# High-half products first in each weight unit, and a sparser accumulating DMA, in a two-layer decoder step

## The chip, the cores and the metric

One core of a Trainium2 chip runs the whole program. The metric is the device time of one execution in microseconds; the kernel before took 1725.13 us as the median of 3 runs (1719.79 to 1726.79). The engines named below are TensorE (PE, its weight loads as PEld), VectorE (DVE), ScalarE (ACT), GpSimd (POOL) and SyncE (SP, which here only issues DMAs).

## The reference, cut to what matters

A step of a decoder with two layers and shared weights runs on 256 prompt tokens and 64 sample tokens, all float32, model width 1024, FFN width 2816:

```
for each layer:
    x = x + 0.5 * swiglu(rmsnorm(x), ffn1_w_gu, ffn1_w_down)
    h = rmsnorm(x)
    u, v, q, gates = split(h @ w_in)
    A = pooling mixer on u              # windows 2, 4, 8, 16, then a 256x256 map per group
    B = conv module on v                # GLU, depthwise conv of width 31, LayerNorm, swish, w_pw
    C = cross-attention of q            # keys and values: rmsnorm(mem) @ w_mem_kv, or a cache
    x = x + (sig(gA)*A + sig(gB)*B + sig(gC)*C) @ w_out
    x = x + 0.5 * swiglu(rmsnorm(x), ffn2_w_gu, ffn2_w_down)
y = rmsnorm(x)
```

Outputs are y for both groups, the new pooling and convolution states, and the memory keys and values of the prompt group.

## The kernel before, in words

**Layout.** Activations lie transposed: features on the 128 partitions, in 8 blocks, and the 256 + 64 = 320 tokens along the free dimension. A weight matrix is cut into blocks of 128 x 128, and the host has put all blocks of both layers into one array in the order of use, so that the kernel reads its weights as a stream. A piece of 16 blocks (1 MB) is one DMA of SP into a tile `raw`, of which there are four (`NRAW`). A piece is two units of 8 blocks, half 0 and half 1.

**Two halves of a number.** PE multiplies in fp32r, which keeps fewer bits than float32. So each float32 operand is cut into a high half, its fp32r rounding, and a low half, the rest, and a product is made of three: weight high by activation high, weight high by activation low, weight low by activation high. The activations' halves are `hhi` and `hlo` (after a norm), `hidh` and `hidl` (FFN hidden), `memh` and `meml` (memory tokens), `mgh` and `mgl` (merged branches) and `chi` and `clo` (convolution); the weights' halves are `whi` and `wlo`.

**Cutting the weights.** `Stream.split` (L211) makes both halves of a unit. The ordinary way (L224): ACT copies `raw` to `whi` with a cast, and DVE writes `wlo` as `raw - whi`; on the profile DVE's instructions carry the line of a helper, L116. The other way (L217 to L219): ACT copies, ACT writes `-raw` cast into `wlo`, and POOL issues a DMA that reads the same weights from HBM once more and adds them into `wlo`. This accumulating DMA is used while `share` is on, for half 1 of each piece: from the start of a layer's mixer to the end of its convolution, 37 of 73 units a layer, 74 of the program's 444 units. When half 1 is cut, the raw tile is given back, and SP may load into it.

**Look-ahead.** `Stream.unit` (L230) is called when PE's program reaches a unit u. It runs deferred work, cuts units up to u + 3 (`LA`), and advances side tasks (`pump`, L268). `whi` and `wlo` have four buffers each (`NW`), so the cut of a unit waits until PE has read the unit four before.

**Chains.** `chain` (L291) makes one output block of 128 features by 320 tokens in a PSUM bank: for each of its 8 blocks (22 in the down projection of the FFN) three matmuls, L294 (`whi` by high), L295 (`whi` by low), L296 (`wlo` by high). A unit of 8 blocks is 24 matmuls. `kv_values` (L456) makes the memory values with weights as the moving operand; there a unit is 12 matmuls of 512 columns at L469 to L471. PSUM has three banks `mm` for chains, two `cv` (shared with the convolution), two `st` and one `sa`; a chain waits until its bank has been read by DVE or ACT.

**Stages of a layer.** `ffn` (22 pairs of gate and up chains, then 8 down chains of 22 blocks); then `mixer`: the GLU projection (16 chains, whose results `za` and `sgv` DVE evicts), the memory keys (8 chains of 256 tokens, evicted by DVE into `kt`), the memory values, the queries, four groups of pooling projection, pool map, pooling gates and attention scores, then attention gates with attention values, convolution gates; then `w_pw` and `w_out`, and the second `ffn`. The last down chain of a stage gives the last of the 8 blocks of x, whose halves the next stage's first chain needs: DVE adds, ACT writes `hhi`, DVE writes `hlo`.

**Side tasks.** The depthwise convolution of the prompt tokens is 240 multiply-adds a layer on DVE (`cv`, two lanes), issued in slices of 2.5 steps a unit from the GLU projection on; for the sample tokens POOL does it. It must be done before `w_pw`. Softmax, pooling and the norms of the mixer are issued in such slices too.

**Order.** Each engine runs its queue in order. The tile framework fixes that order when the program is built: it takes instructions in program order as its own timing model finds them ready, so that a later instruction may be put before an earlier one that the model thinks would wait.

Of the kernel before, what the change touches and what calls it, by code (L numbers as in the profile page):

```python
# [11 lines left out]
ALU = mybir.AluOpType  # L12
# [3 lines left out]
P = 128  # L16
KB = 8
# [58 lines left out]
def trunk_kernel(  # L76
# [16 lines left out]
    nc = tc.nc  # L93
# [9 lines left out]
    clk = {"pe": 0.0, "dve": 0.0, "pool": 0.0}  # L103
# [19 lines left out]
    def nm(s):  # L123
        uid[0] += 1
        return f"{s}_{uid[0]}"
# [4 lines left out]
    def t320(s):  # L130
        return tp.tile([P, T], F32, name=nm(s), tag="t320", bufs=7)
# [4 lines left out]
    def pmm():  # L136
        return psum("mm", 3)
# [7 lines left out]
    def pst():  # L145
        return psum("st", 2)
# [18 lines left out]
    class Stream:  # L165
# [45 lines left out]
        def split(self, u):  # L211
            c, half = divmod(u, 2)
            raw = self.piece("w", c)[:, half * 1024:half * 1024 + 1024]
            hi = wp.tile([P, 1024], F32R, name=nm("whi"), tag="whi")
            lo = wp.tile([P, 1024], F32R, name=nm("wlo"), tag="wlo")
            if self.share and half == 1:
                nc.scalar.copy(hi[:, :], raw)  # L217
                nc.scalar.mul(lo[:, :], raw, -1.0)  # L218
                nc.gpsimd.dma_start(lo[:, :], w_in[c][:, 1024:2048], accum_op=ALU.add)  # L219
            else:  # L220
                n = 512 if u == 0 else 1024
                for e in range(0, 1024, n):
                    h, r = hi[:, e:e + n], raw[:, e:e + n]
                    nc.scalar.copy(h, r)  # L224
                    dve.tensor_tensor(out=lo[:, e:e + n], in0=r, in1=h.bitcast(F32), op=ALU.subtract)
            self.units[u] = (hi, lo)
            if half == 1:
                self.done("w", c)
# [60 lines left out]
    ws = Stream()  # L289

    def chain(out, xs, n):  # L291
        for i, (xh, xl) in enumerate(xs):
            hi, lo = ws.block()
            nc.tensor.matmul(out, hi, xh, start=(i == 0), stop=False)  # L294
            nc.tensor.matmul(out, hi, xl, start=False, stop=False)  # L295
            nc.tensor.matmul(out, lo, xh, start=False, stop=(i == len(xs) - 1))  # L296
            clk["pe"] += 3 * (3 + n / 2.4) * 1e-3


    def rsqrt_ops(ms, n, out, work=None):  # L300
# [60 lines left out]
    def ffn(h, mean, on_block):  # L361
# [12 lines left out]
        for j in range(NJ):  # L374
            pg = pwide()
            chain(pg[:, :T], xs, T)
            sg = t320("sg")

            def ev_gate(pg=pg, sg=sg):
                dve.tensor_tensor(out=sg[:, :], in0=pg[:, :T], in1=rstd[:, :], op=ALU.mult)  # L380
                nc.scalar.activation(sg[:, :], sg[:, :], AF.Silu)

            pu = pwide()
            if j == 0:
                chain(pu[:, :T], xs, T)
                ev_gate()
            else:
                ev_gate()
                chain(pu[:, :T], xs, T)
            up = t320("up")  # L390
            dve.tensor_tensor(out=up[:, :], in0=pu[:, :T], in1=rstd[:, :], op=ALU.mult)
            dve.tensor_tensor(out=up[:, :], in0=up[:, :], in1=sg[:, :], op=ALU.mult)

            def fin(j=j, up=up):
                split_plain(up[:, :], *ref(j))

            defer(fin)
# [58 lines left out]
    def kv_values(l, mh, vt):  # L456
        for half in range(2):
            pv = [pmm(), pmm()]
            for kp in range(4):
                assert ws.blk % 8 == 0  # L460
                hi, lo = ws.unit(ws.blk // 8)
                ws.blk += 8
                for kk in range(2):
                    k = 2 * kp + kk
                    wh, wl = hi[:, kk * 512:kk * 512 + 512], lo[:, kk * 512:kk * 512 + 512]
                    for mb in range(2):
                        sh = mh[0][:, k, mb * P:mb * P + P]
                        sl = mh[1][:, k, mb * P:mb * P + P]
                        nc.tensor.matmul(pv[mb][:, :], sh, wh, start=(k == 0), stop=False)  # L469
                        nc.tensor.matmul(pv[mb][:, :], sl, wh, start=False, stop=False)  # L470
                        nc.tensor.matmul(pv[mb][:, :], sh, wl, start=False, stop=(k == KB - 1))  # L471
                        clk["pe"] += 0.65
            for mb in range(2):
                nc.scalar.mul(vt[:, mb, half * 512:half * 512 + 512], pv[mb][:, :], rmcol[:, mb:mb + 1])
        nc.gpsimd.dma_start(mv_out[l], vt[:, :, :])
# [187 lines left out]
    def mixer(l, h, acc, on_block):  # L663
# [55 lines left out]
        start("norm", norm_gen(), 2)  # L719
        kv_keys(l, mh)  # L720
        kv_values(l, mh, vt)
        drain("norm")
        xs = hx(box[0])
# [168 lines left out]
    for l in range(L):  # L892
# [30 lines left out]
        else:  # L923
            fst = Stat()
            last = t320("sq")
# [9 lines left out]
    m = pst()  # L935
# [114 lines left out]
```

## Time and profile before

| | |
|---|---|
| median of 3 runs | 1725.13 us |
| profiled execution, whole / span | 1725.18 / 1723.4 us |
| PE busy | 1654.5 us (96%) |
| DVE busy | 1119.0 us (65%) |
| ACT busy | 840.7 us (49%) |
| POOL busy | 319.8 us (19%) |
| HBM read, written | 311.91 MB, 8.82 MB |

The span goes from the first to the last instruction; the profiled execution's own time is 1.8 us longer. Times in the views are microseconds from the span's start. In a row, `wlo<-raw,whi` says that an instruction writes `wlo` and reads `raw` and `whi`; `<-` in a list of waits stands between who waited and what ended the wait. Layer 0's mixer lies from about 253 to 580, layer 1's from about 1099 to 1430; the rest is FFN and projections.

### The profile page before, as it was taken

The page shows a single profiled execution, that of the slowest core. Times are in us where ns is not written, and L with a number is a line of the kernel's source. Part 1 is how long each engine was busy: PE and PEld are TensorE (multiplying, and loading weights), DVE is VectorE, ACT ScalarE, POOL GpSimd, SP SyncE. Part 2 cuts the span into 40 slices and gives each one's busy share as a digit, 9 for nine tenths or more (in the row PEclk, how much of TensorE's full clock was granted, in tenths as well). Part 3 has the DMA queues.
Part 4 walks back from the last instruction along what each step waited for, and adds up shares of the span by engine and source line. Part 5 has one row for each costly group of instructions (what it writes and reads, how often), then busy time and mean ns, then how long its engine had stood idle before and what let it go on. Part 6 is the DMA issues. An engine that isn't in the chain of part 4 may idle for free.

```text
span 1723.4 us, 27500 instructions
## 1 busy us (share of the span) xinstructions
PE 1654.5 (96%) x11194; PEld 1597.1 (93%) x11194; DVE 1119.0 (65%) x1822; ACT 840.7 (49%) x1267; POOL 319.8 (19%) x356
## 2 busy tenths in 40 slices
PE   8999998889999999999999999998899999999996
PEld 8999998879788999999999999997888899999996
DVE  7655449999754576564465555689995636755544
ACT  5444346656657354443344433555666664444432
POOL 2000005777410000000000000367762100000000
PEclk9999999999999999999999999999999999999999
DMA  7444457899899544444444444688888974444430
GB/s 266 147 147 152 152 185 214 219 256 253 251 293 273 176 151 155 147 147 148 147 147 150 153 155 154 180 230 230 227 266 269 311 208 161 147 150 154 155 129 31
DMA packets 51935, 322.52 MB, mean 187 GB/s; under 512 B 6240, under 2 KB 6304, under 8 KB 18656
## 3 DMA queue, kind: packets, MB, share of 16 engines
q1 hardware_dynamic: 38160, 270.75, 45.1%
q0 software_dynamic: 13360, 49.68, 13.5%
q8 instruction: 88, 1.44, 0.3%
q10 hardware_dynamic: 288, 0.33, 0.1%
q14 instruction: 39, 0.32, 0.1%
HBM read 311.91 MB, written 8.82 MB: 186 GB/s over the span
## 4 chain that ended last, share of the span: by engine, by line
PE 76%; DMA 9%; DVE 8%; issue 3%; POOL 2%; ACT 2%; DVEq 0%; SPq 0%; POOLq 0%; ACTq 0%
PE mm L296 17%; PE mm L294 17%; PE mm L295 17%; DMA wlo<-in_w 9%; PE cv L294 7%; PE cv L296 7%; PE cv L295 7%; DVE cv L116 3%; POOL pr L116 2%; DVE wlo L116 1%; PE sa L645 1%; DVE us L116 1%; PE st L825 1%; ACT wlo L218 1%; DVE hlo L116 0%
## 5 line engine op out<-in xcount | busy, mean ns | idle before, releaser
L224 ACT CAST whi<-raw 128x1024 fp32r<-128x1024 f32 (+1 forms) x371 | 388.3, 1047 | 601.5 <-PE mm L295 345.2
L116 DVE TENSOR_TENSOR wlo<-raw,whi 128x1024 fp32r<-128x1024 f32 (+1 forms) x371 | 465.3, 1254 | 242.5 <-ACT whi L224 241.6
L294 PE MATMUL mm<-hhi,whi 128*128 128x320 f32 x1736 | 547.0, 315 | 16.1 <-DVE sgv L116 9.6
L296 PE MATMUL mm<-hhi,wlo 128*128 128x320 f32 x1736 | 541.3, 313 | 16.4 <-DMA wlo<-in_w 16.3
L295 PE MATMUL mm<-hlo,whi 128*128 128x320 f32 x1736 | 542.0, 312 | 0.0
L294 PEld LDWEIGHTS mm<-hhi,whi 128*128 128x128 f32 x1736 | 329.3, 190 | 28.2 <-issue 15.5
L296 PEld LDWEIGHTS mm<-hhi,wlo 128*128 128x128 f32 x1736 | 328.9, 190 | 22.0 <-DMA wlo<-in_w 19.9
L295 PEld LDWEIGHTS mm<-hlo,whi 128*128 128x128 f32 x1736 | 329.4, 190 | 1.8 <-issue 0.4
L116 DVE SCALAR_TENSOR_TENSOR cv<-z,cst,cv 128x256 f32<-128x256 f32 x480 | 205.4, 478 | 3.4 <-ACT cv L484 1.4
L294 PE MATMUL cv<-hhi,whi 128*128 128x320 f32 x568 | 175.5, 309 | 0.0
L295 PE MATMUL cv<-hlo,whi 128*128 128x320 f32 x568 | 175.5, 309 | 0.0
L296 PE MATMUL cv<-hhi,wlo 128*128 128x320 f32 x568 | 175.5, 309 | 0.0
L116 POOL MEMSET z<- 128x120 f32 x4 | 0.8, 212 | 742.2 <-PE mm L295 742.2
L217 ACT CAST whi<-raw 128x1024 fp32r<-128x1024 f32 x74 | 77.5, 1048 | 120.3 <-PE mm L295 110.3
L294 PE MATMUL mm<-hidh,whi 128*128 128x320 f32 x418 | 129.2, 309 | 0.0
L295 PE MATMUL mm<-hidl,whi 128*128 128x320 f32 x418 | 129.2, 309 | 0.0
L296 PE MATMUL mm<-hidh,wlo 128*128 128x320 f32 x418 | 129.2, 309 | 0.0
L116 POOL TENSOR_TENSOR pr<-pr 128x512 f32<-128x512 f32 (+3 forms) x128 | 116.6, 911 | 6.6
L219 POOL DMA_DIRECT2D wlo<-in_w x74 | 64.6, 873 | 257.8 <-ACT wlo L218 188.5
L296 PEld LDWEIGHTS cv<-hhi,wlo 128*128 128x128 f32 x568 | 106.6, 188 | 0.0
L295 PEld LDWEIGHTS cv<-hlo,whi 128*128 128x128 f32 x568 | 106.6, 188 | 0.0
L294 PEld LDWEIGHTS cv<-hhi,whi 128*128 128x128 f32 x568 | 106.6, 188 | 0.0
(191 smaller groups left out, 2632.0 us busy)
## 6 DMA issues: line engine op xcount, KB each, us to landing
raw<-in_w SPq DMA_DIRECT2D x221, 1024.0 KB, 4.8
wlo<-in_w POOLq DMA_DIRECT2D x74, 512.0 KB, 8.9
raw<-in_kc SPq DMA_DIRECT2D x16, 1024.0 KB, 9.3
raw<-in_vc SPq DMA_DIRECT2D x16, 1024.0 KB, 8.7
out_co<-z POOLq DMA_DIRECT2D x16, 135.0 KB, 6.0
raw<-in_mem SPq DMA_DIRECT2D x2, 1024.0 KB, 4.8
out_mk<-kt POOLq DMA_DIRECT2D x2, 1024.0 KB, 9.4
out_mv<-va POOLq DMA_DIRECT2D x2, 1024.0 KB, 8.3
```

The costliest lines, as they stand in the source:

```text
L116: return op(*args, **kw)
L217: nc.scalar.copy(hi[:, :], raw)
L218: nc.scalar.mul(lo[:, :], raw, -1.0)
L219: nc.gpsimd.dma_start(lo[:, :], w_in[c][:, 1024:2048], accum_op=ALU.add)
L224: nc.scalar.copy(h, r)
L294: nc.tensor.matmul(out, hi, xh, start=(i == 0), stop=False)
L295: nc.tensor.matmul(out, hi, xl, start=False, stop=False)
L296: nc.tensor.matmul(out, lo, xh, start=False, stop=(i == len(xs) - 1))
L645: nc.tensor.matmul(po[32 * h:32 * h + 32, :256], pp[:, at:at + 32], raw[:, mb * 1024 + h * 256:mb * 1024 + h * 256 + 256], start=(bb == 0 ...
L825: nc.tensor.matmul(pv[:, :TP], vt[:, mb, o * P:o * P + P], kt[:, 2 * hd + mb, :], start=(mb == 0), stop=(mb == 1))
```

## The change

It has two parts. In `chain`, the blocks of one unit (or as many of them as belong to the chain) are taken together: first L294 and L295 for all of them, then L296 for all of them; `kv_values` does the same with its units. In `Stream.split`, the accumulating DMA is used, while `share` is on, for every unit whose number leaves 2 when divided by 3, whichever half it is, and no longer for each half 1.

```diff
--- before.py
+++ after.py
@@ -213,10 +213,10 @@
             raw = self.piece("w", c)[:, half * 1024:half * 1024 + 1024]
             hi = wp.tile([P, 1024], F32R, name=nm("whi"), tag="whi")
             lo = wp.tile([P, 1024], F32R, name=nm("wlo"), tag="wlo")
-            if self.share and half == 1:
+            if self.share and u % 3 == 2:
                 nc.scalar.copy(hi[:, :], raw)
                 nc.scalar.mul(lo[:, :], raw, -1.0)
-                nc.gpsimd.dma_start(lo[:, :], w_in[c][:, 1024:2048], accum_op=ALU.add)
+                nc.gpsimd.dma_start(lo[:, :], w_in[c][:, half * 1024:half * 1024 + 1024], accum_op=ALU.add)
             else:
                 n = 512 if u == 0 else 1024
                 for e in range(0, 1024, n):
@@ -289,12 +289,18 @@
     ws = Stream()
 
     def chain(out, xs, n):
-        for i, (xh, xl) in enumerate(xs):
-            hi, lo = ws.block()
-            nc.tensor.matmul(out, hi, xh, start=(i == 0), stop=False)
-            nc.tensor.matmul(out, hi, xl, start=False, stop=False)
-            nc.tensor.matmul(out, lo, xh, start=False, stop=(i == len(xs) - 1))
-            clk["pe"] += 3 * (3 + n / 2.4) * 1e-3
+
+        i, last = 0, len(xs) - 1
+        while i <= last:
+            m = min(8 - ws.blk % 8, last + 1 - i)
+            blocks = [(xs[i + e], ws.block()) for e in range(m)]
+            for e, ((xh, xl), (hi, lo)) in enumerate(blocks):
+                nc.tensor.matmul(out, hi, xh, start=(i + e == 0), stop=False)
+                nc.tensor.matmul(out, hi, xl, start=False, stop=False)
+            for e, ((xh, xl), (hi, lo)) in enumerate(blocks):
+                nc.tensor.matmul(out, lo, xh, start=False, stop=(i + e == last))
+            clk["pe"] += 3 * m * (3 + n / 2.4) * 1e-3
+            i += m
 
 
     def rsqrt_ops(ms, n, out, work=None):
@@ -460,16 +466,15 @@
                 assert ws.blk % 8 == 0
                 hi, lo = ws.unit(ws.blk // 8)
                 ws.blk += 8
-                for kk in range(2):
-                    k = 2 * kp + kk
-                    wh, wl = hi[:, kk * 512:kk * 512 + 512], lo[:, kk * 512:kk * 512 + 512]
-                    for mb in range(2):
-                        sh = mh[0][:, k, mb * P:mb * P + P]
-                        sl = mh[1][:, k, mb * P:mb * P + P]
-                        nc.tensor.matmul(pv[mb][:, :], sh, wh, start=(k == 0), stop=False)
-                        nc.tensor.matmul(pv[mb][:, :], sl, wh, start=False, stop=False)
-                        nc.tensor.matmul(pv[mb][:, :], sh, wl, start=False, stop=(k == KB - 1))
-                        clk["pe"] += 0.65
+                w4 = [(kk, mb) for kk in range(2) for mb in range(2)]
+                for kk, mb in w4:
+                    k, wh = 2 * kp + kk, hi[:, kk * 512:kk * 512 + 512]
+                    nc.tensor.matmul(pv[mb][:, :], mh[0][:, k, mb * P:mb * P + P], wh, start=(k == 0), stop=False)
+                    nc.tensor.matmul(pv[mb][:, :], mh[1][:, k, mb * P:mb * P + P], wh, start=False, stop=False)
+                for kk, mb in w4:
+                    k, wl = 2 * kp + kk, lo[:, kk * 512:kk * 512 + 512]
+                    nc.tensor.matmul(pv[mb][:, :], mh[0][:, k, mb * P:mb * P + P], wl, start=False, stop=(k == KB - 1))
+                    clk["pe"] += 0.65
             for mb in range(2):
                 nc.scalar.mul(vt[:, mb, half * 512:half * 512 + 512], pv[mb][:, :], rmcol[:, mb:mb + 1])
         nc.gpsimd.dma_start(mv_out[l], vt[:, :, :])
```

## Rows read from the trace of the kernel before

**Rows 1.** Windows by stage: busy us (instructions) per engine, clock, DMA share, GB/s.
```profile
253.00:372.00 119.00, 103.64 (x638) 96.79 (x637) 110.83 (x211) 70.57 (x110) 76.99 (x81) 0.94 0.81 219
372.00:580.00 208.00, 199.79 (x1422) 179.42 (x1421) 142.32 (x276) 132.05 (x233) 73.50 (x85) 1.00 0.89 263
580.00:1099.00 519.00, 519.00 (x3536) 518.52 (x3535) 302.58 (x428) 215.78 (x291) 2.83 (x5) 1.00 0.43 152
1099.00:1218.00 119.00, 101.58 (x631) 95.55 (x630) 109.51 (x202) 67.35 (x100) 79.39 (x85) 0.94 0.82 221
1218.00:1430.00 212.00, 202.87 (x1426) 182.77 (x1425) 139.78 (x267) 131.96 (x233) 71.45 (x76) 0.98 0.86 255
```

**Rows 2.** PE's waits from 253 to 372: total us, times, longest us.
```profile
PE mm L294 <- DVE sgv L116: 5.5, 2, 3.8
PE mm L296 <- DMA wlo<-in_w: 5.3, 4, 2.7
PE mm L471 <- DMA wlo<-in_w: 3.2, 1, 3.2
PE mm L294 <- DVE kt L116: 1.3, 1, 1.3
```

**Rows 3.** PE's waits from 372 to 580.
```profile
PE mm L296 <- DMA wlo<-in_w: 5.7, 5, 2.2
```

**Rows 4.** PE's waits from 1099 to 1218.
```profile
PE mm L296 <- DMA wlo<-in_w: 4.7, 2, 2.6
PE mm L294 <- DVE sgv L116: 4.0, 2, 3.8
PE mm L471 <- DMA wlo<-in_w: 3.3, 2, 2.2
PE mm L296 <- DVE wlo L116: 2.9, 1, 2.9
PE mm L294 <- DVE kt L116: 2.2, 1, 2.2
```

**Rows 5.** PE's waits from 1218 to 1430.
```profile
PE mm L296 <- DMA wlo<-in_w: 7.7, 6, 2.6
```

**Rows 6.** Windows on five stretches of lower granted clock.
```profile
326.10:329.50 3.40, 3.40 (x18) 3.40 (x17) 3.40 (x9) 1.65 (x3) 1.94 (x3) 0.50 1.02 222
356.80:363.60 6.80, 5.59 (x13) 4.38 (x14) 6.76 (x14) 3.83 (x7) 4.97 (x3) 0.50 0.66 183
...
1141.90:1145.20 3.30, 3.30 (x14) 3.30 (x13) 0.00 (x0) 0.00 (x0) 2.50 (x3) 0.50 0.94 228
1179.50:1186.20 6.70, 3.98 (x18) 3.98 (x19) 6.70 (x10) 0.00 (x0) 1.58 (x1) 0.50 0.74 214
1397.90:1404.70 6.80, 6.18 (x23) 6.18 (x24) 0.47 (x1) 0.18 (x1) 0.00 (x0) 0.50 0.82 212
```

**Rows 7.** Timeline of one accumulating unit: start us, us, engine, line, operation.
```profile
1388.16 0.85 POOL L219 DMA_DIRECT2D wlo<-in_w  x1 [13.49 <-ACT exo L653]
...
1398.52 0.63 PE L296 MATMUL mm<-hhi,wlo 128*128 128x320 f32 x1 [2.58 <-DMA wlo<-in_w]
```

**Rows 8.** Part 6 of the page, DMA issues: KB each, median us to landing.
```profile
wlo<-in_w POOLq DMA_DIRECT2D x74, 512.0 KB, 8.9
```

**Rows 9.** DVE groups, 253 to 372: count, busy us, mean ns, idle.
```profile
L116 DVE SCALAR_TENSOR_TENSOR cv<-z,cst,cv 128x256 f32<-128x256 f32 x126 | 54.4, 477 | 1.2 <-ACT cv L484 0.7
L116 DVE TENSOR_TENSOR wlo<-raw,whi 128x1024 fp32r<-128x1024 f32 x16 | 24.2, 1513 | 3.7 <-ACT whi L224 3.5
```

**Rows 10.** Groups of DVE from 20 to 250, the first FFN.
```profile
L116 DVE TENSOR_TENSOR wlo<-raw,whi 128x1024 fp32r<-128x1024 f32 x65 | 79.5, 1223 | 39.8 <-ACT whi L224 39.7
```

**Rows 11.** Groups of DVE from 1099 to 1218.
```profile
L116 DVE SCALAR_TENSOR_TENSOR cv<-z,cst,cv 128x256 f32<-128x256 f32 x134 | 57.1, 478 | 1.2 <-ACT cv L484 0.7
```

**Rows 12.** Timeline where the second FFN of layer 0 begins.
```profile
625.99 0.31 PE L294 MATMUL cv<-hhi,whi 128*128 128x320 f32 x1
...
628.33 0.55 DVE L116 SCALAR_TENSOR_TENSOR hlo<-x,cst,hhi 128x320 fp32r<-128x320 f32 x1
```


## The prediction

> **What bounds the kernel now.** I read the busy time by stage first, then who TensorE (PE) waited for in each stage, then the clock in the stretches after the long waits, then VectorE's (DVE's) costliest groups. By stage [rows 1] there are two kinds of time. In the FFN, and in the pointwise and output projections, PE is busy all of the time: 519.00 of 519.00 us, 3536 matmuls, 0.147 us from start to start. There nothing but PE's own work counts, and that work is the same after the change: same matmuls, same weight loads, other order. In the two mixers PE leaves holes. I cut each mixer in an early part (GLU projection, memory keys, memory values; 119 us each) and a late part (queries to the branch gates; 208 and 212 us). In the early parts DVE is the fullest engine beside PE, 110.83 and 109.51 of 119; in the late ones it has room, 142.32 of 208 and 139.78 of 212.
>
> The holes, by cause: the low half of a weight unit (wlo) that had not landed from its accumulating DMA cost 5.3 + 3.2 us in the first early part [rows 2], 5.7 in the first late part [rows 3], 4.7 + 3.3 in the second early part, where DVE's own wlo was 2.9 late as well [rows 4], and 7.7 in the second late part [rows 5]. That is 8.5, 5.7, 10.9 and 7.7: 32.8 us of waiting for a low half. The rest are evictions (sgv 5.5 and 4.0, kt 1.3 and 2.2), which the change does not touch directly.
>
> Such holes are paid twice. After several of them the granted clock is 0.50, which is 1.2 of 2.4 GHz [rows 6]: in the stretch at 1397.90, which follows the longest late wait, 23 matmuls took 6.18 busy us, 0.269 each against 0.147. So of 6.8 us at the low level about 45% is lost, 3.0 us.
>
> **The change part by part.**
>
> *Order inside a unit.* A unit of 8 blocks is now 16 products with the high half, then 8 with the low. Before, the first low product was third; now it is seventeenth: the low half may come 14 starts, 14 x 0.147 = 2.1 us, later. The last reader of the high half was the 23rd product, now it is the 16th: ScalarE's copy of the unit four ahead, which waits for that buffer, may start 7 starts, 1.0 us, earlier; its negated copy into wlo still waits for the low buffer, whose release does not move, but comes at once then. Together up to 3.1 us of slack for an accumulating unit. In one such unit [rows 7] POOL's issue took 0.85 us from 1388.16 and the low product came 10.4 us after it, 2.6 of them waited; the median from issue to landing is 8.9 us [rows 8]. For the key units (256 columns) I scale the cadence: 0.147 x 256/320 = 0.117, an estimate, so 1.6 + 0.8 = 2.4 us; for the value units (512 columns, 12 matmuls, low product from 3rd to 9th, high half free 3 starts earlier) 0.235, so 1.4 + 0.7 = 2.1 us. Against the longest waits, 2.7, 3.2 and 2.2 [rows 2, 4], about 1.5 us stays; the late ones, 2.6 at most [rows 5], are covered whole.
>
> *Every third unit.* From 37 accumulating units in a mixer to 24: 13 fewer each, 26 in all, so 13.3 MB less on the DMA queues (512 KB each [rows 8]), which are 0.81 to 0.89 busy there [rows 1], and 26 fewer POOL issues of 0.85 and as many ScalarE passes, both off the path. Instead DVE makes 26 more subtractions. The early part has 15 accumulating units of 32 before and 10 after: 5 more subtractions in each, at 1.51 us [rows 9], 7.5 us of DVE. The late part gets 8 more, about 10 us, into 66 or 72 us of DVE idle: nothing. Half-1 units that DVE now makes give their raw tile back after the subtraction rather than after ScalarE's pass, which moves SP's next load by a microsecond or two; the load has four raw tiles, seven units or some 24 us, and costs nothing.
>
> The early subtractions are dear: 1513 ns there [rows 9], 1223 in the FFN [rows 10], while POOL is busy 77 to 79 of 119 us there and nearly idle in the FFN [rows 1]. The Trainium skill (SBUF — State Buffer, Who interferes with whom) says that a DVE instruction with two SBUF inputs contends with a GpSimd instruction that reads SBUF, and both inputs of this subtraction are in SBUF; the trace agrees, and without that rule 5 of them would be 6.1 us and not 7.5.
>
> *Late parts.* All low waits go, 5.7 + 7.7 = 13.4 us, and the slow stretch at 1397.90 with them, 3.0: **16.4 us gained**. Bounds: half of it, 8 us, if waits for raw tiles or ScalarE come up behind; 16.4.
>
> *Early parts.* Low waits 8.5 + 10.9 less the 1.5 that stays are 17.9; the slow stretches after waits that contain a low half (3.40, 6.80, 3.30 and 6.70 us in [rows 6]) at 45% are 9.1. So PE alone would gain 27. But DVE sets the floor: 110.8 + 7.5 = 118.3 of today's 119 in the first, 109.5 + 7.5 = 117.0 in the second, before any idle. The convolution, which fills DVE's gaps, can be left for the late part as far as the low half's slack allows; the second mixer is a little ahead with it (134 steps against 126 at the end of the early part [rows 9, 11], 8 x 0.43 = 3.4 us). I take no gain in the first, 4 us in the second, **4 us**. Bounds: all 27, if DVE puts off its convolution; 15 lost, if both times 7.5 lands on the path.
>
> *Chains that begin a stage.* The last x block of a new stage is now wanted as products 15 and 16 of its first chain, not 22 and 23. In one such boundary [rows 12] the chain begins at 625.99, and the last hlo is ready at 628.33 + 0.55 = 628.88; PE would now ask for it at 625.99 + 15 x 0.147 = 628.19, 0.7 us early, where before it asked at 629.22. There are seven such boundaries and the program's start. PE may slip products of the next chain into that hole: between 0 and 8 x 0.7 = 5.6 us; I take **2 us lost**.
>
> *Sum.* 1725.2 (the profiled run, 1.8 us of it around its span of 1723.4) - 16.4 - 4 + 2 = 1706.8. The median of the runs is 1725.1, so no correction: **1707 us**, 1.1% faster. Its own range is 1697 to 1717.
>
> **The rivals.**
>
> *DVE becomes the bound of the early parts (slower).* Each high copy gets its subtraction late, keys wait for their PSUM bank longer than the 1.3 and 2.2 us of today [rows 2, 4]. For it: DVE at 93% there, and one DVE wlo already 2.9 late. Against: 9 us of its idle in each, and the convolution can wait. It decides when DVE's backlog passes what three PSUM banks bear, two key chains or 2 x 24 x 0.117 = 5.6 us; 7.5 us are added. Price: 15 us on the path, four more slow stretches of 6.8 us at 3.0 = 12, boundaries 5.6, against 16.4 in the late parts: 1725.2 + 15 + 12 + 5.6 - 16.4 = 1741.
>
> *Something else is late next (no change).* The low half waits no more, but raw tiles, ScalarE's copies and POOL's queue come out just behind it. For it: DMA 0.89 and 0.86 busy in the late parts [rows 1]. Against: 13 MB less traffic. Half of the late gain, nothing early: 1725.2 - 8 + 2 = 1719.
>
> *DVE has room (faster still).* The convolution drifts into the late parts and PE gets all: 1725.2 - 16.4 - 27 + 2 = 1684. For it: 66 and 72 us of DVE idle late. Against: DVE works in order, and the convolution's steps stand in its queue ahead of later subtractions.
>
> **How the numbers follow.** Forecast 0.46, no change 0.21, faster still 0.20, slower rival 0.13. About 0.5%, 8.6 us, is what a measurement here can tell from none. Faster by that (below 1716.5): nine tenths of the forecast, all of the faster rival, a fifth of the second: 0.66. Slower (above 1733.7): most of the slower rival, 0.12. Within: 0.22. The range leaves out a part of the rivals at either end: 1685 to 1730.
>
> **What would show it.** Right: waits of PE for DMA wlo under 5 us in all, no granted clock of 0.50 near the end of the second mixer, late parts of about 202 us each, DVE busier than 117 us in early parts that are no shorter than 115, FFN stages unchanged to 1 us. Wrong: late parts as long as before with another wait in place (then the second rival), early parts longer with waits for kt, sgv or DVE's wlo (the first), early parts near 105 us (the third), or holes of over 1 us where a stage begins.

## The result and the profile after

The kernel after took 1701.78 us (median of 4 runs, 1697.46 to 1705.72) against 1725.96 (4 runs): a ratio of 0.986 [0.983, 0.990]. The profiled execution took 1699.24 us, 25.9 less than that of before. The forecast of 1707 us was 5 us above the measured median. How the gain is made up is not what the prediction said, so that nearness is in good part luck.

The accumulating DMA in part 6 of the page after (KB each, median us to landing, as [rows 8]); 26 fewer, as reckoned, and sooner there (7.7 in a second profile of the same program, e7 below):

```profile
wlo<-in_w POOLq DMA_DIRECT2D x48, 512.0 KB, 7.0
```

For the stages I divided both traces where PE ends one and begins the next: GLU projection, keys with values, late part, then all between the mixers, and the first three again for the second mixer. The columns are those of [rows 1]. First after, then before, divided in the same way:

```profile
245.40:311.10 65.70, 59.55 (x391) 58.64 (x390) 59.41 (x108) 37.46 (x62) 29.22 (x33) 0.97 0.67 197
311.10:366.60 55.50, 50.16 (x292) 44.69 (x291) 51.64 (x93) 30.23 (x46) 35.63 (x37) 0.91 0.77 229
366.60:563.40 196.80, 189.03 (x1358) 171.82 (x1357) 157.15 (x293) 124.40 (x224) 80.07 (x84) 0.98 0.78 246
563.40:1085.40 522.00, 522.00 (x3558) 521.68 (x3557) 303.14 (x434) 216.18 (x293) 1.91 (x4) 1.00 0.43 151
1085.40:1148.80 63.40, 59.04 (x389) 58.27 (x388) 56.77 (x102) 34.55 (x54) 34.89 (x39) 0.97 0.69 204
1148.80:1200.70 51.90, 47.82 (x289) 41.99 (x288) 50.80 (x91) 30.87 (x47) 38.54 (x38) 0.97 0.82 245
1200.70:1393.90 193.20, 188.52 (x1357) 170.24 (x1356) 153.44 (x285) 123.81 (x221) 70.79 (x74) 0.99 0.79 250
```

```profile
245.60:312.60 67.00, 60.04 (x393) 58.84 (x392) 57.51 (x112) 39.62 (x65) 34.68 (x40) 0.97 0.79 216
312.60:376.00 63.40, 54.36 (x314) 47.87 (x312) 58.78 (x114) 37.20 (x53) 46.91 (x47) 0.92 0.84 227
376.00:569.10 193.10, 185.84 (x1333) 166.41 (x1334) 131.37 (x256) 125.06 (x224) 69.81 (x81) 1.00 0.89 263
569.10:1091.70 522.60, 522.29 (x3558) 521.70 (x3557) 308.12 (x435) 216.62 (x292) 1.92 (x4) 1.00 0.43 153
1091.70:1159.40 67.70, 60.96 (x389) 59.80 (x388) 55.13 (x109) 36.87 (x55) 39.55 (x45) 0.95 0.78 209
1159.40:1221.00 61.60, 50.91 (x308) 45.59 (x308) 58.78 (x104) 34.45 (x50) 40.75 (x41) 0.94 0.86 236
1221.00:1418.70 197.70, 189.28 (x1338) 169.74 (x1338) 129.82 (x251) 127.14 (x227) 71.45 (x76) 0.98 0.86 256
```

One trap lies in this division, and the matmul counts show it: the late parts have 1333 and 1338 matmuls before and 1358 and 1357 after. In the kernel before, a query chain's 24 and some 19 matmuls ran already among the values, at 0.147 us worth 3.5 and 2.8 us. At equal work the early parts (GLU to values) went from 130.4 - 3.5 = 126.9 to 121.2 and from 129.3 - 2.8 = 126.5 to 115.3: 5.7 and 11.2 us gained. The late parts went from 196.6 to 196.8 and from 200.5 to 193.2: 0.2 lost and 7.3 gained. The rest of the program is 1.9 shorter. Together 16.9 + 7.1 + 1.9 = 25.9.

These gains hold for this pair of executions. A second profile of the kernel after (e7) has early parts of 126.4 and 113.6 us and late parts of 197.2 and 193.7: 0.5 and 12.9 us gained early, 0.6 lost and 6.8 gained late.

PE's waits after, over the whole span (who waited, what ended it: total, times, longest), beside [rows 2 to 5]:

```profile
PE mm L298 <- ACT ut L767: 7.9, 4, 3.9
PE mm L476 <- DMA wlo<-in_w: 6.4, 3, 3.3
...
PE mm L299 <- DVE pll L116: 1.8, 1, 1.8
...
PE mm L301 <- DMA wlo<-in_w: 1.1, 3, 0.5
```

The 32.8 us of waiting for a low half have become 7.5. In the chains (L301) it is almost gone. What is left lies among the values (L476), where a unit is 12 matmuls. The longest of these waits, 3.29 us, has its beginning in POOL's queue (start us, us, engine, line, operation, idle time before it and what ended that):

```profile
344.27 1.06 ACT L218 ACTIVATE wlo<-raw 128x1024 fp32r<-128x1024 f32 x1
...
347.44 0.87 POOL L219 DMA_DIRECT2D wlo<-in_w  x1
...
357.49 2.08 PE L476 MATMUL mm<-wlo,memh 128*128 128x512 f32 x4 [3.29 <-DMA wlo<-in_w]
```

ScalarE was done with the unit at 345.33, but POOL was working on its convolution of the sample tokens (`pr`) and issued the DMA 2.1 us later. In the second mixer the value unit that PE waited 2.46 us for was issued 3.9 us after ScalarE's end, again behind `pr`.

New in place of the waits for low halves are pool maps (L298) that wait for ScalarE's copy `ut` (7.9), where before one such wait of 0.7 stood. The granted clock shows it as well. The first of the late parts' stretches at 1.2 GHz comes right after the longest of these waits:

```profile
427.90:431.30 3.40, 3.40 (x24) 1.78 (x23) 3.34 (x5) 2.21 (x5) 2.88 (x2) 0.50 0.00 0
```

The stretch at 1397.90 [rows 6] is gone, but three of 3.4 us have come (at 427.9, 492.8 and 1305.1): 10.2 us against 6.8. Where the new wait comes from is seen in the timeline ahead of the first, and in the same place of the kernel before:

```profile
421.65 0.68 DVE L116 TENSOR_REDUCE mx<-st 128x2 f32<-128x512 f32 x1
...
423.45 1.28 ACT L587 ACT_TABLE_LOAD   x1 [4.29 <-DVE mx L116]
...
426.60 0.43 ACT L767 COPY ut<-mm 128x320 f32<-128x320 f32 x1
...
427.08 0.42 PE L298 MATMUL mm<-plh,whi 128*128 128x320 f32 x1 [3.94 <-ACT ut L767]
```

```profile
425.79 0.68 DVE L116 TENSOR_REDUCE mx<-st 128x2 f32<-128x512 f32 x1
...
428.04 1.28 ACT L582 ACT_TABLE_LOAD   x1 [4.41 <-DVE mx L116]
...
431.67 0.41 PE L294 MATMUL mm<-plh,whi 128*128 128x320 f32 x1 [0.67 <-ACT ut L762]
```

ScalarE's queue stood 4.29 us for the softmax maximum `mx` of DVE; behind it lay the copy `ut`, which frees the PSUM bank that PE's next pool map wants. ScalarE's wait is not new: it was 4.41 us before, and cost PE only 0.67. What is new is that DVE lies further behind PE. From the first matmul of these scores (421.20 before, 413.33 after) to `mx` pass 4.6 us before and 8.3 after. In that time DVE makes nine steps of the convolution before and ten after; what has come on top is a subtraction (1.35 us), two of the pooling's operations on `us` (0.78 and 0.18) and a longer `pll` (2.02 for 1.12). Over the whole mixer, convolution steps moved too, which the windows on DVE's `cv` steps show (busy us, count), before and then after, first mixer:

```profile
245.60:312.60 67.00, 24.08 (x54) 0.97 0.79 216
312.60:376.00 63.40, 34.38 (x84) 0.92 0.84 227
376.00:569.10 193.10, 48.50 (x114) 1.00 0.89 263
```

```profile
245.40:311.10 65.70, 21.57 (x47) 0.97 0.67 197
311.10:366.60 55.50, 25.08 (x61) 0.91 0.77 229
366.60:563.40 196.80, 61.15 (x143) 0.98 0.78 246
```

In the early part 138 steps became 108 (143 became 116 in the second mixer), in the late part 114 became 143 (109 became 136). So DVE, which gets more subtractions early, was not busier there: 57.51 + 58.78 = 116.3 us of 130.4 before, 59.41 + 51.64 = 111.1 of 121.2 after.

### The profile page after: what moved, and what is told of

Read it like the earlier page. It is cut to its first block, busy times and chain, and to the rows that moved or that the text cites. A ratio compares the mean times of both kernels' runs of the same rounds, so it can differ in the third digit from the quotient of the medians.

```text
span 1697.5 us, 27410 instructions
## 1 busy us (share of the span) xinstructions
PE 1646.4 (97%) x11194; PEld 1594.0 (94%) x11194; DVE 1146.7 (68%) x1848; ACT 821.2 (48%) x1241; POOL 305.9 (18%) x330
## 4 chain that ended last, share of the span: by engine, by line
PE 77%; DVE 16%; issue 3%; DMA 2%; ACT 2%; POOL 1%; DVEq 0%; SPq 0%; POOLq 0%; ACTq 0%
PE mm L298 17%; PE mm L299 17%; PE mm L301 17%; PE cv L301 7%; PE cv L299 7%; PE cv L298 7%; DVE cv L116 6%; DVE wlo L116 4%; DVE us L116 2%; DMA wlo<-in_w 2%; PE sa L650 1%; PE st L830 1%; DVE rx L116 1%; POOL pr L116 1%; DVE ysum L116 1%
## 5 line engine op out<-in xcount | busy, mean ns | idle before, releaser
L116 DVE TENSOR_TENSOR wlo<-raw,whi 128x1024 fp32r<-128x1024 f32 (+1 forms) x397 | 505.4, 1273 | 193.2 <-PE mm L301 81.6
L224 ACT CAST whi<-raw 128x1024 fp32r<-128x1024 f32 (+1 forms) x397 | 414.7, 1045 | 406.0 <-PE mm L299 231.7
L298 PE MATMUL mm<-hhi,whi 128*128 128x320 f32 x1736 | 522.2, 315 | 16.5 <-DVE sgv L116 10.5
L299 PE MATMUL mm<-hlo,whi 128*128 128x320 f32 x1736 | 519.4, 313 | 0.0
L298 PEld LDWEIGHTS mm<-hhi,whi 128*128 128x128 f32 x1736 | 328.7, 189 | 27.9 <-issue 12.4
L301 PE MATMUL mm<-hhi,wlo 128*128 128x320 f32 x1736 | 293.4, 310 | 0.3 <-DMA wlo<-in_w 0.3
L301 PEld LDWEIGHTS mm<-hhi,wlo 128*128 128x128 f32 x1736 | 264.8, 188 | 1.0 <-DMA wlo<-in_w 0.6
L298 PE MATMUL cv<-hhi,whi 128*128 128x320 f32 x568 | 167.8, 309 | 0.0
L298 PE MATMUL mm<-hidh,whi 128*128 128x320 f32 x418 | 123.7, 309 | 0.0
L354 ACT CAST hidh<-up 128x320 fp32r<-128x320 f32 x88 | 40.0, 459 | 164.1 <-DVE up L116 164.1
L298 PEld LDWEIGHTS cv<-hhi,whi 128*128 128x128 f32 x568 | 106.6, 188 | 0.0
L301 PE MATMUL cv<-hhi,wlo 128*128 128x320 f32 x568 | 94.8, 309 | 0.0
L116 DVE TENSOR_TENSOR up<-mm,rstd 128x320 f32<-128x320 f32 x54 | 26.5, 490 | 88.6 <-PE mm L301 88.6
L301 PEld LDWEIGHTS cv<-hhi,wlo 128*128 128x128 f32 x568 | 86.2, 188 | 0.0
L298 PE MATMUL cv<-hidh,whi 128*128 128x320 f32 x286 | 84.6, 309 | 0.0
```

What stands on the lines that cost most here:

```text
L116: return op(*args, **kw)
L298: nc.tensor.matmul(out, hi, xh, start=(i + e == 0), stop=False)
L301: nc.tensor.matmul(out, lo, xh, start=False, stop=(i + e == last))
L354: nc.scalar.copy(hi, src)
```

## The experiments

My theory after this reading: the order's slack and the thinner accumulating DMA both take away waits for the low half; the early parts got shorter than DVE's busy time allowed since the convolution is free to move; and what moved is what PE waits for late. The last of these is a guess: the timeline above does not show it. The main rival: DVE is the floor of the early parts all the same, so whoever gives it more work there loses. Edits are against the kernel after where nothing else is said.

**Each part alone.** The new order with the old choice of units (e1), and the old order with every third unit (e2: `chain` and `kv_values` as before).

```diff
-            if self.share and u % 3 == 2:
+            if self.share and half == 1:
```

> The order of the products alone; the accumulating DMA stays at half 1 of every piece. Theory A (the order carries the gain: a low half that comes up to 2.1 us late no longer stops PE): PE's waits for wlo from the DMA fall from 30 us to under 10, and the time is 1700 to 1710 us. Theory B (the sparser DMA carries it: fewer low halves are late at all): waits for wlo still above 15 us, time above 1717. Under A the late parts of the mixers should be shorter than in the changed kernel, because DVE has 13 fewer subtractions a mixer, and the waits of the pool maps (plh on ACT ut, 8 us in the changed kernel) should be under 4 us.

> Every third unit on the accumulating DMA, with the products in the old order. Theory A: each of the 48 low halves is still wanted at the third product, so waits for wlo fall only in proportion to their count or a little more, from 30 to 12 to 20 us, and DVE's added subtractions bring the pool maps' waits of some 8 us: 1712 to 1724. Theory B: waits for wlo under 8 us, time under 1708.

e1: 1709.65 us, ratio 0.993 [0.991, 0.994]; e2: 1709.27 us, 0.992 [0.991, 0.994]. PE's waits of e1, then of e2:

```profile
PE mm L476 <- DMA wlo<-in_w: 5.7, 3, 4.0
PE mm L298 <- ACT ut L767: 5.5, 2, 3.6
...
PE mm L301 <- DMA wlo<-in_w: 3.5, 3, 2.7
```

```profile
PE mm L294 <- ACT ut L762: 5.5, 4, 2.6
PE mm L296 <- DMA wlo<-in_w: 4.9, 4, 2.9
PE mm L471 <- DMA wlo<-in_w: 4.9, 2, 2.7
```

Each part alone takes the wait for the low half from 29.9 us (the share of the 32.8 that DMAs ended) to 9.2 and 9.8, and each brings 0.75%; together they bring 1.36%. For e2 I had expected less, 1712 to 1724. Thirteen fewer accumulations a mixer were thus worth as much as the order, which the prediction had not seen. The waits for `ut` come with either part.

In e1 two things that I expected did not come. The waits for `ut` stayed above 4 us, and the late parts (198.2 and 192.5 us, with 17 and 24 matmuls of the queries done ahead of them) were not shorter than those of the kernel after (196.8 and 193.2), although DVE was busy for only 134.6 and 129.9 us there, against 157.2 and 153.4. More work of DVE in the late part is therefore not needed for these waits. Among the values e1 still waits 5.7 us, where the kernel before waited 6.5: the order alone did little there.

**No accumulation at all** (e3), DVE makes every low half.

```diff
-            if self.share and u % 3 == 2:
+            if False:
```

> The new order, and no accumulating DMA at all: DVE makes all low halves, 24 more subtractions a mixer than the changed kernel (about 31 us of DVE each). If DVE's backlog is what limits the changed kernel's late parts: early parts get DVE-bound, waits for sgv, kt, pool maps and DVE's wlo above 30 us, time above 1725. If DVE had room: no wait for a DMA is left, and the time is 1690 to 1700.

1701.05 us, 0.988 [0.986, 0.990], as fast as the kernel after. The windows of its first mixer, keys with values and late part:

```profile
311.50:359.00 47.50, 45.61 (x291) 41.36 (x290) 47.50 (x74) 26.54 (x44) 34.84 (x30) 1.00 0.53 184
359.00:557.80 198.80, 191.26 (x1358) 172.28 (x1358) 181.98 (x334) 111.84 (x210) 77.51 (x74) 0.98 0.58 212
```

Here DVE is busy for 47.50 of 47.50 us, and the stage is 8.0 us under the kernel after. In the second mixer it takes 51.8 us against 51.9, with DVE busy for 50.5: nothing gained there, and nothing lost. A full DVE is no floor as long as part of what fills it can wait. The rival falls: who gives DVE more work there does not lose. It is the late part that is long here, 198.8 us with DVE 182 busy (201.7 in the second mixer).

**Which third** (e4): other units, 25 a mixer in place of 24.

```diff
-            if self.share and u % 3 == 2:
+            if self.share and u % 3 == 0:
```

> The changed kernel with the accumulating DMA at units whose number leaves 0, not 2, when divided by 3: the same count and order, other units, and another order of the queues where the framework's timing model decides otherwise. If the gain is of the mechanism and not of one lucky order: 1697 to 1711 with waits for wlo under 10 us. If it is luck: above 1715.

1709.48 us, 0.992 [0.990, 0.995], 8 us above the kernel after; the two intervals touch. Its waits:

```profile
PE mm L298 <- ACT ut L767: 12.8, 4, 5.8
PE mm L476 <- DMA wlo<-in_w: 8.9, 2, 6.5
```

Three accumulating units lie in the first value stage instead of two, and one of them stops PE for 6.5 us; POOL issued it 4.3 us after ScalarE's part was done, behind `pr` again. Which units are chosen counts, though one more of them lies in the early part as well, and no run separates the two.

**The kernel after once more** (e7, no edit), since differences of this size were to be read.

> The changed kernel again, on the same chip as its variants, to compare them with: ratio 0.986, as before, so 1697 to 1702.

1698.13 us (1694.13 to 1703.43), 0.987 [0.984, 0.990]. It is the same program, and yet its runs span 9 us. Single stages of one execution are therefore good to a few us only: the early part of the first mixer takes 126.4 us here and 121.2 above, with 23.9 us of it at the lower clock against 13.7, which at 45% is 4.6 of the 5.2.

**Accumulating only late (e5) or only early (e6).** A layer has 222 units; 98 lie ahead of the queries.

```diff
-            if self.share and u % 3 == 2:
+            if self.share and u % 3 == 2 and u % 222 >= 98:
```

> The changed kernel with the accumulating DMA only in the late part of each mixer (from the queries on); in the early part DVE makes all low halves, 5 x 2 more than half of what the kernel without any accumulating DMA adds. Theory C (the early part is held by late low halves from the DMA, not by DVE, since the convolution is put off into the late part): early parts as in the kernel without it, key and value stages of 48 and 52 us, no wait for wlo in the value stage; late parts 195 to 200 us; in all 1693 to 1701. Theory D (DVE's work is a floor of the early parts): key and value stages of 58 us or more, time above 1705.

> The other half of that: the accumulating DMA for every third unit only in the early part, DVE makes all low halves in the late part. Theory C: early parts as in the changed kernel (key and value stages 55 and 52 us, waits for wlo of some 6 us in the value stage), late parts as without any accumulating DMA (199 and 202 us), because DVE's backlog delays the pool maps there: 1703 to 1711. Theory D: late parts unchanged from the changed kernel (197 and 193), time 1698 to 1703.

e5: 1689.49 us (1686.85 to 1691.11), 0.982 [0.979, 0.984], better than expected, and below both kernels. e6: 1701.46 us, 0.989 [0.985, 0.993]. The same two windows of e5:

```profile
311.40:359.00 47.60, 45.72 (x292) 41.43 (x292) 47.60 (x77) 27.37 (x45) 34.98 (x30) 1.00 0.52 183
359.00:553.90 194.90, 189.28 (x1357) 170.16 (x1356) 164.52 (x316) 124.11 (x224) 84.72 (x89) 0.99 0.82 257
```

The early part is that of e3, 113.9 us, and the late parts, 194.9 and 190.6 us, are shorter than those of e3 by 3.9 and 11.1. So accumulating DMAs cost early, where a low half is wanted soon and DVE can put something off: e6, which has them there alone, takes 121.1 and, at equal work, 120.3 us for its early parts, where e5 takes 113.9 and 114.9. That they help late is not shown. e6 has none there, and its late parts took 191.4 and, at equal work, 197.6 us (195.2 with 16 matmuls of the queries done earlier), with 3.0 of waits for `ut`; in sum that is 3.5 us more than e5 and 11.5 less than e3. Its time lies in the range of the theory that e5 refutes. One difference from e3 is on record: e6 has as much to subtract late, but did more of the convolution in its longer early parts (146 and 138 steps left against 167 and 156), so DVE is busy there for 170 and 169 us and not 182 and 180. Put-off work alone does not decide either: e5 has more convolution left than the kernel after (164 and 153 steps against 143 and 136), and waits for `ut` only 2.0. What stands ahead of `mx` and `ut` in each program's queues is the likelier reason, not traced here.

**Convolution issued more slowly (e8), and half of it left out (e9).**

```diff
-RC = 2.5
+RC = 2.2
```

```diff
-            for k in range(1, TAPS):
+            for k in range(1, 16):
```

> The changed kernel with the convolution issued in 2.2 instead of 2.5 steps a unit, so that fewer of its steps stand ahead of the pooling, the softmax and the subtractions in DVE's queue. Theory C (DVE's backlog of convolution steps holds ScalarE's queue and through it the pool maps): waits of the pool maps (plh on ACT ut, pll on DVE), 9.7 us in the changed kernel, fall under 5, late parts under 193 us, time 1690 to 1698, unless the convolution ends too late and PE waits before the pointwise projection. If the pool maps are late for another reason (POOL's own work, ScalarE's load): no change, 1697 to 1704.

> The changed kernel with only 15 of the 30 multiply-adds of each convolution block on DVE (the prompt's convolution is left half done): 120 fewer DVE instructions of 0.43 us a mixer, nearly all of them out of the late part. If DVE's put-off convolution is what holds the pool maps, the softmax and ScalarE's queue in the late parts: waits of the pool maps (9 us) and of the scores fall under 3 us in all, late parts 186 to 190 us each (197 and 193 now), early parts as now, time 1680 to 1690. If those waits have another source (POOL's work, ScalarE's own load, the order of the queues): waits of the pool maps stay above 6 us and the time is above 1692.

e8: 1716.32 us, 0.997 [0.995, 1.000]; e9: 1699.68 us, 0.986 [0.982, 0.990]. The waits of e8, then of e9:

```profile
PE mm L298 <- ACT ut L767: 9.7, 5, 4.0
...
PE mm L298 <- ACT chi L572: 6.8, 2, 3.4
```

```profile
PE mm L298 <- DVE sgv L116: 16.3, 7, 3.9
PE mm L298 <- DVE kt L116: 11.0, 3, 5.6
```

e8 missed: the `ut` waits did not shrink, and the convolution came too late for `w_pw`, which waits for `chi`. In e9 the `ut` waits are gone, as expected, and the late parts take 192.8 and 185.3 us, the second with 17 matmuls fewer, so 187.8 at equal work. The expected 186 to 190 holds for one of them; both are below the kernel after. That shows, by taking half of them away, that the convolution's steps in DVE's queue are needed for those waits; how few fewer would do, it does not show. The total was a miss, for the early parts became longer, 128.7 and, at equal work, 119.0 us: `sgv` and `kt` now came late, with DVE's operations themselves stretched (last section).

**How thick the late accumulations may be (e10), and whether the order still matters with them late only (e11; `chain` and `kv_values` as before).** e10:

```diff
-            if self.share and u % 3 == 2:
+            if self.share and half == 1 and u % 222 >= 98:
```

> The accumulating DMA only in the late parts, and there on half 1 of each piece, 21 units a mixer instead of 15. If the late part is held by DVE's load: late parts 1 to 4 us shorter than with every third, time 1683 to 1689. If the denser DMA makes low halves late again: waits for wlo above 6 us, time 1690 to 1698.

> Every third unit on the accumulating DMA in the late parts alone, with the products in the old order: what the order is still worth when the early parts have no such DMA. If the order carries a gain of its own in the late parts: low halves wait again for 5 to 10 us there and the time is 1696 to 1704. If it only covered what the sparser DMA removes anyway: 1688 to 1694.

e10: 1712.54 us, 0.993 [0.991, 0.995]; e11: 1708.38 us, 0.993 [0.991, 0.996]. Both above what either theory had. The waits of e10, with its DMA issues, then the waits of e11:

```profile
PE mm L301 <- DMA wlo<-in_w: 5.3, 4, 3.1
...
wlo<-in_w POOLq DMA_DIRECT2D x44, 512.0 KB, 9.9
```

```profile
PE mm L296 <- DMA wlo<-in_w: 6.1, 4, 2.7
...
PE mm L296 <- DVE wlo L116: 2.3, 1, 2.3
```

Every second late unit (22 a mixer) in place of every third (15) costs 23 us against e5 (20 by the ratios): the landing takes 9.9 us where e5 has 8.0, and the late parts take 204.6 and 206.1 us, 25.2 more in the two. The waits of the low half account for 2 of these. All listed waits of the late parts are 24.8 us against 9.5, and 23.9 us lie at the lower clock against 3.4, which at 45% cost 9.2: together 24.5 of the 25.2. The waits that came are of many kinds (scores, softmax, `ut`, `merged`), so the first cause among them stays open. e11 says that the order is worth 19 us beside e5 too, and that it covers more than DMAs: its early parts, which have none of these DMAs, take 119.0 and 115.6 us against 113.9 and 114.9, and one of DVE's own low halves is 2.3 late there.

**The better version with another third** (e12), to see whether e5 is a lucky choice of units as the kernel after against e4 was.

```diff
-            if self.share and u % 3 == 2:
+            if self.share and u % 3 == 0 and u % 222 >= 98:
```

> The accumulating DMA only in the late parts, for the units whose number leaves 0 instead of 2: as fast a version in another order of the queues. Early parts are the same as with remainder 2 (GLU 66 and 63, keys and values 48 and 52 us). If the late part's 195 and 191 us come from the density of the DMA and the product order: within 4 us of them, time 1686 to 1697. If they hang on which units go by DMA, as the changed kernel's 8 us between remainder 2 and 0 suggest: late parts 198 us or more each, time 1698 to 1706.

1690.94 us, 0.982 [0.980, 0.984]: within 1.5 us of e5. The gain of accumulating late only does not hang on the phase. The stages do not bear out the expectation behind it: the late parts took 199.7 and 194.9 us in the profiled execution (1693.65 us), more than 4 us above those of e5 (profiled at 1686.85), and the early parts 113.8 and 112.3. The choice of units still moves single stages.

## Why the prediction was right and where it was wrong

*What bounds the kernel.* Right: PE was stopped by low halves, and stages without such waits did not change (522.6 to 522.0 us between the mixers).

*"Order inside a unit"*, slack of 3.1 us. Right for the chains: 1.1 us of waits is left. Wrong for the values, where 6.4 stayed and not 1.5: the longest wait there is still 3.3 us. The prediction took POOL's issues to be off the path. Among the values they are on it: in the two longest waits the issue stood 2.1 and 3.9 us behind POOL's own `pr`, as much as the slack or more, and 4.3 in e4's wait of 6.5.

*"Every third unit"*. The step priced DVE's subtractions and gave the 13 MB less of DMA no price at all. That term was missing: landing fell from 8.9 to 7.0 us (7.7 in e7), the DMA share late from 0.89 and 0.86 to 0.78 and 0.79, and this part alone (e2) removed two thirds of the waits and brought as much as the order alone (e1). The two overlap in what they remove, though their gains nearly add. The count was off by one as well: an early part has 9 accumulating units after, not 10 (e6 has 18 in two), so 6 more subtractions, 9.1 us at 1.51, and not 7.5.

*"Late parts", 16.4 gained.* This step failed in its size: the waits for the low half went as said (12.4 us in this division, 0.3 after), but 7.1 came, 6.2 by e7. PE waits 9.7 us for `ut` and `pll` instead, and has 10.2 us at the lower clock for 6.8. That is the second rival's kind, something else late next: of the three that it named (raw tiles, ScalarE's copies, POOL's queue), a copy of ScalarE, held up by DVE. All listed waits of the late parts went from 16.5 to 12.4 us, and 3.4 more at the lower clock cost 1.5: 2.6 of the 7.1. The other 4.5 are not assigned.

*"Early parts: DVE sets the floor", 4 gained.* This step failed in its reason: 16.9 came, 13.4 by e7. Waits of 32.4 us became 19.7, and stretches at the lower clock 27.2 us became 20.5, at 45% another 3.0; that is 15.7 of the 16.9. The prediction added 7.5 us of subtractions to DVE's busy time as if all of it had to be done there, though it named the way out, a convolution that drifts, as the third rival. DVE's busy time fell by 5 and 6 us while it got the additional subtractions. e3 and e5 show it at the extreme, with DVE full among the keys and values of the first mixer. The prediction's objection, that DVE works in order and the convolution's steps stand ahead of what is wanted later, did not keep the early gain away. In the late part those steps do matter, as e9 shows.

*"Chains that begin a stage", 2 lost.* No wait of that kind appeared, and the stretch between the mixers, with such boundaries in it, got no longer; the term is nothing.

So the errors, 9 too much late and 13 too little early, nearly cancelled, and that is why the total came near: luck, not the sum. Of the signs named, the lower clock in the second mixer's end and unchanged FFN stages came; low waits under 5 us in all (7.5), a DVE busy for more than 117 us in the early parts (111.1 and 107.6), and late parts shorter in both mixers did not. The second rival's sign, a late part as long as before with another wait in place, came in the first mixer.

*What stays open:* why programs with nearly the same number of accumulations (48 and 50) differ by 8 us beyond the value stage; how far e6's late parts are short because of its convolution alone; which wait comes first in e10's late parts; where 4.5 of the 7.1 us gained late come from.

## What to carry to other kernels

Before an engine's busy time is taken as a floor of a stage, subtract what it does there that is not due there; the put-off work is then to be followed to its due place, and to the queue that it will hold up. When an operand is late, ask for it later within the same accumulation, or make fewer such transfers: here each brought 0.75% and both together 1.4%, and keeping the extra DMAs out of the tight stage 0.5% more. A variant that depends on how a program's order falls should be tried in a second phase (e4, e12) before its gain is believed.

## What the runs showed of the hardware

Two-input operations of DVE stretch beside POOL. With half the convolution gone (e9), POOL did more of its own work early, 85.5 of 128.7 us busy against 64.9 of 121.2. DVE's subtractions there took longer on the mean (line, operation, count, busy us, mean ns) than the 1223 ns of the FFN [rows 10], where POOL is nearly idle:

```profile
L116 DVE TENSOR_TENSOR wlo<-raw,whi 128x1024 fp32r<-128x1024 f32 x22 | 38.1, 1734 | 4.8 <-ACT whi L224 4.2 <-PE mm L301 0.6
```

In the kernel after the mean over the same stage is 1536 ns. They do not all stretch alike: of the 22 in e9 the fastest took 1207 ns, the median 1380 and the slowest 3303. A smaller operation in e9, `rx`, shows it one by one. It takes 0.41 us on 256 columns when it is alone, but two of them took over 2 us, each at the same time as POOL's `pr`:

```profile
313.04 2.18 DVE L116 TENSOR_TENSOR rx<-rx,rx 128x256 f32<-128x256 f32 x1
...
313.33 1.59 POOL L116 TENSOR_TENSOR pr<-pr 128x512 f32<-128x512 f32 x1
```

No run took POOL's work away alone, so the cause is argued from the company that these operations keep. The Trainium skill (SBUF — State Buffer, Who interferes with whom) names that company: two SBUF inputs on DVE against a GpSimd instruction that reads SBUF; these numbers agree, and operations of DVE that read PSUM did not move (`za` 475 and 476 ns).

The landing of the same 512 KB accumulating DMA ranged from 6.8 us (e6, 18 of them) to 9.9 (e10, 44 of them, all late). Two profiles of the kernel after had 7.0 and 7.7, so smaller differences say nothing. Their number alone does not set it, since e1 has 74 and 8.9. How thick they stand goes with it: in the late parts the median was 8.7 to 10.3 us where every second unit accumulates (before, e1, e10), and 6.3 to 8.5 where every third does (after, e2, e4, e5, e7 to e9, e11, e12).
